# A hybrid decoder layer: value products that read two rows in turn, and tokens copied into residue order

## The chip, the cores and the metric

The kernel runs on one core of a Trainium2 chip. A core has five engines, each of which works through its own list of instructions strictly in order: TensorE (PE; the loading of its stationary operand is shown apart as PEld), VectorE (DVE), ScalarE (ACT), GpSimd (POOL) and SyncE (SP, which here only issues transfers). An instruction may wait for semaphores that other engines or transfers raise; what stands behind it on its list waits with it. SBUF is the on-chip memory that all engines read, PSUM the eight banks in which TensorE accumulates. The metric is the time of one execution on the device, in microseconds, lower is better.

## The reference, cut to what matters

One decoder layer on 512 tokens of width 1024, in float32: half a SwiGLU feed-forward step, a token mixer, and another half feed-forward step, each between RMS norms.

```python
def token_mixer(h, ...):
    proj = h @ w_in                      # all queries, keys, values and gates
    o_nsa = nsa_attention(...)           # 8 heads, 2 key groups: compressed, selected and window branches
    o_dil = dilated_attention(...)       # 12 heads: 3 groups with dilation 1, 4 and 16
    y = sigmoid(g_a) * (o_nsa @ w_nsa_o) + sigmoid(g_b) * (o_dil @ w_dil_o)
    return y @ w_mix_out
```

In `nsa_attention` each head's output is a gated sum of three attentions; each is a product of probabilities and values, `p @ v`. In `dilated_attention` position t of group g reads the tokens t, t-d, t-2d, ... with d = 1, 4 or 16; the groups' outputs are added with weights that come from the softmax denominators of all three.

## The kernel before

**Precision.** Each float32 operand is split into a rounded high part and a low remainder (`split`, L163 on ScalarE and L164 on VectorE); a product is three matmuls, high x high, high x low, low x high (`mm3`, L208 to L210). Weights arrive in `raw` buffers by SP's queue and are split into `whi` and `wlo`, 1024 columns at a time. The tokens stand transposed in `xhl_t`, eight k-tiles of 128 features by 512 tokens, high and low.

**In turn.** With `turn=True` `mm3` reads the moving operand as two rows, the first and second half of its columns, one element of each in turn, and writes the results to the bank one after the other, so that the bank holds the two rows interleaved. Who reads the bank undoes that (`from_turn`). The value products did not do so.

**NSA.** For each of 8 heads and 2 branches the scaled probabilities are transposed to (keys x queries), split, and `hb_values` (L1290) multiplies the value tile of each of four key tiles with them, 512, 384, 256 and 128 queries wide (causal), high and low, into one PSUM bank V. The compressed branch is added by L1364, 512 wide. `fold` (L1298 on ScalarE, L1299 on VectorE) adds the two halves of the bank's partitions into the head's output.

**Dilated attention and the block products.** The dilated scores and softmax rows (L1013, L1014 on TensorE, L1019 on VectorE, L1020 on ScalarE) run between seven-product block multiplications ("P1" to "P7") of the tokens with other columns of `w_in`; a table, PLAN, says how many blocks follow each half head. In the last of four lots P6, P7 and P4 share a T bank in turn: the first has its bank copied to a `ring` buffer by L1539, the second by L1551, and only then P4 may accumulate into the bank on top of it; L1633 keeps P4.

**Dilated values.** The first group's values are projected token tile by token tile (until 632 us) and kept high and low by L1756 and L1757. Groups 2 and 3 need the tokens by residue modulo 4: the projection's stationary operand is `xhl_t` read with a step of four elements, token tile t being residue t. Eight k-tiles, four banks (S, S, T, T), three matmuls each: 96 matmuls 512 wide, which I call the residue stage. During it `factors` computes the groups' weights (L1719 to L1734), and GpSimd scales the dilated probabilities with them (L1747). Then, for each of 4 heads and 3 groups, the probabilities are transposed (L1799 or L1812), split into SP buffers, and multiplied: group 1 by L1826 and L1827 into bank V, copied by L1828; groups 2 and 3 by L1834, 256 columns at a time, added by L1839.

**What sets the order.** The kernel is written as one stream of operations; the framework's scheduler sets the list of each engine by when it reckons operands and buffers are ready. Buffers come from named pools of fixed number: SP has 11 buffers of 128 x 512, used among others for the low parts of splits; a new use waits until all readers of the old one are done.

Of the kernel before, what the change touches and what calls it, by code (L numbers as in the profile page):

```python
# [13 lines left out]
F32R = mybir.dt.float32r  # L14
# [7 lines left out]
P = 128  # L22
D = 1024
S = 512
# [60 lines left out]
class Layer:  # L85
# [110 lines left out]
    def halves(self, v):  # L196

        return v.rearrange("p (h a c) -> p h a c", h=2, a=2)

    def rows_of(self, v):  # L200

# [1084 lines left out]
    def hb_values(self, probs, br, half, out, first):  # L1286
        for kk in range(NT):
            v = self.vn[kk][:, 2 * br + half].rearrange("p h d -> p (h d)")
            for pi, pp in enumerate(probs[kk]):
                self.nc.tensor.matmul(out[:, kk * P:S], v, pp, start=first and kk == 0 and pi == 0, stop=False,  # L1290
                                      skip_group_check=True)

    def fold(self, dst, half, top, bot):

# [6 lines left out]
    def nsa(self, fillers, sums):  # L1301
        nc = self.nc
        pe = self.positions()
        r = self.wcols([(C_KC, 256)])
        src = [r[:, :, 0:P], r[:, :, P:2 * P]]
        r2 = self.wcols([(C_KS, P), (C_KW, P)])
        src2 = [r2[:, :, 0:P], r2[:, :, P:2 * P]]
        early = []
        for s, tag in zip(src + src2, "FFSV"):
            w = None  # L1310
            if tag == "V":
                with self.tc.issue_after(self.scaled[2]), self.tc.issue_after(self.cast_T[1]):
                    w = self.wslots(s, ["SP"] * 4)
            early.append(self.proj_T(s, self.bank(tag), (0, 2 * P), w))
            if len(early) in (2, 3):
                self.pending.pop(0)()
        for n, (b, w) in enumerate(early):
            self.proj_T(None, b, (2 * P, S), w)
        self.positions_T(pe)
        rows = [self.block_rows(b) for b, _ in early[:2]]  # L1320
        kw = early[3][0]
        vw = self.v_weights()
        kparts = [self.k_parts(early[2][0], False)]
        gs = [self.blocks(0, rows[0])]
        kparts.append(self.k_parts(kw, False))
        gs.append(self.blocks(1, rows[1]))
        wq = self.wslots(self.wcols([(0, 64), (256, 64)]), ["Q", "Q", "of", "of"])
        self.v_nsa(vw)
        early = self.hidden_early(0)
        self.oh, self.ol = [], []  # L1330
        heads = [(i, half, br) for i in range(4) for half in range(2) for br in range(2)]
        qs, cmps, ws, live = {}, {}, {}, {}
        probs = {}
        for n in range(len(heads) + LAG):
            if n < len(heads) and n % 4 == 0:
                i = n // 4
                b, _ = self.proj_T(None, None, None, wq) if i == 0 else self.proj_T(self.wcols([(i * 64, 64), (256 + i * 64, 64)]))
                qs[i] = self.q_parts(b)
                if i:
                    cmps[i] = self.cmp_pair(i, qs[i])  # L1340
            m = n - LAG
            if m >= 0:
                i, half, br = heads[m]
                with self.tc.issue_after(self.unit_mm) if m == 0 else ExitStack():
                    probs[m] = self.hb_probs(*live.pop(m), self.gate[:, :, (i + 4 * half) * 3 + 1 + br])
            if n < len(heads):
                i, half, br = heads[n]
                h = i + 4 * half
                if br == 0:
                    ws[h] = self.slot("W")  # L1350
                    nc.vector.tensor_scalar(ws[h], self.dm, -(2.0 ** -(h + 1)), None, op0=OP.mult)
                kb, ka = kparts[br]
                live[n] = self.hb_scores(qs[i][half], ka[half], kb, half, ws[h])
            if m >= 0:
                i, half, br = heads[m]
                with self.tc.issue_after(self.last_pool):
                    sums(m)
                if br == 0:
                    out = self.bank("V")
                    if half == 0:  # L1360
                        of = self.slot("x")
                self.hb_values(probs.pop(m), br, half, out, br == 0)
                if br == 1:
                    nc.tensor.matmul(out, self.vcs[half], cmps[i], start=False, stop=True, skip_group_check=True)  # L1364
                    self.fold(of, half, out[0:64], out[64:128])
                    if half == 1:
                        self.oh.append(of)
            if n < 2:
                self.hidden(n, gs[n], early)
                if n == 0:  # L1370
                    early = self.hidden_early(1)
                else:
                    hid = self.gelu()
            if n == 2:
                self.compressed(hid)
                cmps[0] = self.cmp_pair(0, qs[0])
            fillers()
# [180 lines left out]
    def dil(self, fillers, early_gates):  # L1558
# [216 lines left out]
        for k0 in range(0, KT, 2):  # L1775
            if k0 % 4 == 0:
                r = self.raw(wv[:, k0:k0 + 4], [4, S])
            w = self.wsplit(r[:, k0 % 4:k0 % 4 + 2], [2, S])
            if k0 == 2:
                factors()  # L1780
            for j in range(2):
                xs = [x[k0 + j].rearrange("p (n r) -> p r n", r=4) for x in (self.xh, self.xl)]
                for t in range(NT):
                    self.mm3(banks[t], xs[0][:, t], xs[1][:, t], w[0][:, j], w[1][:, j], k0 + j == 0, k0 + j == KT - 1,
                             turn=True)
# [3 lines left out]
        def value(g, t, hh):  # L1789
            return vt[g][t][:, hh].rearrange("p h d -> p (h d)")  # L1790
# [29 lines left out]
        def values(g, hh, pieces, acc):  # L1820

            mm = nc.tensor.matmul
            if g == 0:
                out = self.bank("V")
                for n, (kk, qc, hi, lo) in enumerate(pieces):
                    mm(out[:, qc], value(g, kk, hh), hi, start=n == 0, stop=False, skip_group_check=True)  # L1826
                    self.last_value = mm(out[:, qc], value(g, kk, hh), lo, start=False, stop=n == NT - 1, skip_group_check=True).ins  # L1827
                nc.scalar.copy(acc, out)  # L1828
                return
            for m, both in enumerate(pieces):  # L1830
                out = self.bank("S")
                for n in range(2):
                    c = slice(n * 256, (n + 1) * 256)
                    self.last_value = mm(out[:, c], value(g, 2 * m + n, hh), both[:, n].rearrange("p x q -> p (x q)"), start=True,  # L1834
                                         stop=True).ins
                av = acc.rearrange("p (n r) -> p n r", r=4)[:, :, 2 * m:2 * m + 2]
                ov = out.rearrange("p (r x n) -> p x n r", r=2, x=2)
                for x in range(2):
                    nc.vector.tensor_add(av, ov[:, x], av)  # L1839

# [362 lines left out]
```

## Time and profile before

| | before |
|---|---|
| median of 3 runs (lowest to highest) | 1083.85 us (1083.21 to 1085.04) |
| profiled execution, its own time | 1083.9 us |
| span in the trace | 1081.8 us |
| TensorE busy, share of the span | 1060.2 us, 98% |
| VectorE busy | 915.0 us, 85% |
| ScalarE busy | 667.9 us, 62% |
| GpSimd busy | 246.4 us, 23% |
| mean granted TensorE clock | 0.999 |

A row of the timeline gives start, duration, engine, line, operation, tiles written and read, size and count, and in brackets the engine's idle time just before and what ended it. A row of the groups gives the line, the operation, its tiles and sizes, the count, the busy time in us and the mean duration in ns, then the idle time before. A row of the waits gives who waited for whom: us in total, how often, the longest. Matmuls overlap in the pipeline, so their pace is read from the distance of their starts and not from their duration.

| stretch, us | what runs | TensorE busy | VectorE | ScalarE |
|---|---|---|---|---|
| 391 to 510 | NSA heads, with projections between | 114.96 of 119 | 94.57 | 85.48 |
| 510 to 600 | dilated scores and block products | 87.72 of 90 | 78.67 | 69.78 |
| 600 to 633 | last blocks, first value projection | 32.44 of 33 | 20.35 | 22.65 |
| 633 to 656 | residue stage | 23.00 of 23 | 12.12 | 8.91 |
| 656 to 700 | dilated value products | 41.59 of 44 | 35.93 | 27.55 |
| 700 to 1082 | gates, mixer output, second feed-forward | 374.80 of 382 | 323.74 | 209.26 |

### The profile page before, as it was taken

How to read it: one execution, taken by the hardware profiler on the slowest of the kernel's cores; microseconds unless marked ns; L12 is line 12 of the kernel's file. 1: busy time of each engine (PE TensorE's matmuls, PEld its weight loads, DVE VectorE, ACT ScalarE, POOL GpSimd, SP SyncE). 2: the span in 40 equal slices, each digit the busy share in tenths (PEclk: the TensorE clock that was granted, in tenths of full speed). 3: DMA queues.
4: the chain of work that ended last, by engine and by line, in shares of the span. 5: the costliest groups of instructions: out<-in, count | busy, mean ns of one | idle time of the engine just before them, and what ended most of it. 6: DMA issues, size and time to landing. Idle time of an engine off the chain costs nothing. (4 is left out here: it accounts for less than half of the span.)

```text
span 1081.8 us, 19360 instructions
## 1 busy us (share of the span) xinstructions
PE 1060.2 (98%) x7166; PEld 974.6 (90%) x7166; DVE 915.0 (85%) x1563; ACT 667.9 (62%) x1196; POOL 246.4 (23%) x345
## 2 busy tenths in 40 slices
PE   9999999999999999999999999999999999999997
PEld 7899999988889977777899998888999999998886
DVE  6999999998787988787996746996888999989775
ACT  7465555567675777676797745754445555668462
POOL 0434445410021054454110039001101111000001
PEclk9999999999999999999999999999999999999999
DMA  9899999999962577886766642574387988579862
GB/s 351 259 273 312 284 299 294 303 315 351 355 225 87 195 263 174 263 187 204 166 196 224 206 119 99 180 263 162 131 276 203 261 248 229 152 248 301 301 203 105
DMA packets 87871, 250.65 MB, mean 232 GB/s; under 512 B 11777, under 2 KB 16993, under 8 KB 85089
## 3 DMA queue, kind: packets, MB, share of 16 engines
q1 hardware_dynamic: 67152, 180.40, 48.4%
q0 software_dynamic: 20192, 68.72, 25.5%
q8 instruction: 56, 0.92, 0.3%
q10 hardware_dynamic: 432, 0.30, 0.1%
q14 instruction: 39, 0.31, 0.1%
HBM read 214.73 MB, written 74.50 MB: 267 GB/s over the span
## 5 line engine op out<-in xcount | busy, mean ns | idle before, releaser
L164 DVE TENSOR_TENSOR wlo<-raw,whi 128x1024 fp32r<-128x1024 f32 (+1 forms) x216 | 261.8, 1217 | 79.9 <-ACT whi L163 77.2
L163 ACT CAST whi<-raw 128x1024 fp32r<-128x1024 f32 (+1 forms) x216 | 223.8, 1040 | 95.3 <-PE pb_F L209 17.2
L208 PE MATMUL pb_F<-xhl_t,whi 128*128 128x256 f32 (+1 forms) x320 | 104.7, 327 | 2.0 <-DVE KA_s L996 1.0
L209 PE MATMUL pb_F<-xhl_t,whi 128*128 128x256 f32 (+1 forms) x320 | 103.1, 322 | 0.0
L210 PE MATMUL pb_F<-xhl_t,wlo 128*128 128x256 f32 (+1 forms) x320 | 103.1, 322 | 0.0
L208 PE MATMUL pb_S<-xhl_t,whi 128*128 128x256 f32 (+1 forms) x280 | 82.2, 294 | 0.0
L209 PE MATMUL pb_S<-xhl_t,whi 128*128 128x256 f32 (+1 forms) x280 | 82.1, 293 | 0.0
L210 PE MATMUL pb_S<-xhl_t,wlo 128*128 128x256 f32 (+1 forms) x280 | 82.1, 293 | 0.0
L229 POOL TENSOR_TENSOR rs_t<-rs_t,mhalf_t 128x1 f32<-128x1 f32 x20 | 13.3, 666 | 249.5 <-DVE rs_t L225 249.5
L208 PEld LDWEIGHTS pb_F<-xhl_t,whi 128*128 128x128 f32 x320 | 61.0, 191 | 6.1 <-issue 1.6
L210 PEld LDWEIGHTS pb_F<-xhl_t,wlo 128*128 128x128 f32 x320 | 61.0, 190 | 3.3
L209 PEld LDWEIGHTS pb_F<-xhl_t,whi 128*128 128x128 f32 x320 | 61.0, 191 | 3.0 <-issue 0.2
L1266 POOL TENSOR_SCALAR SP_s<-SP_s,st_t 128x384 f32<-128x384 f32 (+2 forms) x48 | 49.1, 1053 | 55.5 <-PE pb_T L1232 11.6
L209 PE MATMUL pb_T<-xhl_t,whi 128*128 128x256 f32 x216 | 59.4, 275 | 0.0
L210 PE MATMUL pb_T<-xhl_t,wlo 128*128 128x256 f32 x216 | 59.4, 275 | 0.0
L208 PE MATMUL pb_T<-xhl_t,whi 128*128 128x256 f32 x216 | 59.4, 275 | 0.0
L163 ACT CAST whi<-tmp_t 128x1024 fp32r<-128x1024 f32 x36 | 36.5, 1057 | 30.2 <-DVE tmp_t L582 26.6
L210 PEld LDWEIGHTS pb_S<-xhl_t,wlo 128*128 128x128 f32 x280 | 53.6, 191 | 1.3
L208 PEld LDWEIGHTS pb_S<-xhl_t,whi 128*128 128x128 f32 x280 | 53.6, 191 | 1.3
L209 PEld LDWEIGHTS pb_S<-xhl_t,whi 128*128 128x128 f32 x280 | 53.6, 191 | 1.3
L208 PE MATMUL pb_T<-SP_s,whi 128*128 128x256 f32 x176 | 48.8, 277 | 1.5 <-ACT ring_s L1539 1.0
L210 PE MATMUL pb_T<-SP_s,wlo 128*128 128x256 f32 x176 | 48.7, 277 | 0.0
(930 smaller groups left out, 3713.4 us busy)
## 6 DMA issues: line engine op xcount, KB each, us to landing
raw<-in_gu_dram SPq DMA_DIRECT2D x64, 512.0 KB, 5.8
raw<-tdram SPq DMA_DIRECT2D x40, 512.0 KB, 5.0
PT_s<-in_d_dram POOLq DMA_DIRECT2D x66, 256.0 KB, 6.9
raw<-in_d_dram SPq DMA_DIRECT2D x30, 512.0 KB, 5.1
tdram<-in_d_dram POOLq DMA_DIRECT2D x18, 768.0 KB, 10.4
ldram<-in_w_in_dram POOLq DMA_DIRECT2D x12, 1024.0 KB, 10.5
tdram<-PT_s POOLq DMA_DIRECT2D x44, 256.0 KB, 5.9
raw<-in_w_in_dram SPq DMA_DIRECT2D x11, 1024.0 KB, 4.9
```

What stands on the lines that cost most here:

```text
L163: self.last_cast = self.nc.scalar.copy(dsthi, src).ins
L164: self.last_sub = self.nc.vector.tensor_sub(dstlo, src, dsthi.bitcast(F32)).ins
L208: mm(out, lhi, rhi, start=start, stop=False, skip_group_check=skip)
L209: mm(out, lhi, rlo, start=False, stop=False, skip_group_check=skip)
L210: self.last_mm = mm(out, llo, rhi, start=False, stop=stop, skip_group_check=skip).ins
L229: nc.gpsimd.tensor_tensor(out=r, in0=v, in1=self.mhalf, op=OP.pow)
L1266: self.last_pool = nc.gpsimd.tensor_scalar(pp, pp, st[:, 1, t:t + 1], None, op0=OP.mult).ins
```

## The change

1. **NSA value products in turn.** The moving probabilities of each 128-column token tile are read as two rows of 64 in turn, and the bank V takes them so; `fold` reads the bank with a step of two and writes its output in natural order.
2. **Dilated value products in turn.** Group 1 likewise. For groups 2 and 3 the two 128-wide pieces of a 256-column product are the two rows; the adds read the bank with a step of two.
3. **Tokens copied into residue order.** For each k-tile of the residue stage ScalarE copies the high and the low tokens into an SP buffer each, reading with a step of four elements and writing contiguously: 16 copies of 128 x 512. The 96 matmuls take the copies as their stationary operand.

```diff
+    def tiles_in_turn(self, v):
+        return v.rearrange("p (t a c) -> p t c a", a=2, c=64)
+    def tiles_turned(self, v):
+        return v.rearrange("p (t c a) -> p t c a", a=2, c=64)
+    def tiles_from_turn(self, v):
+        return v.rearrange("p (t c a) -> p t a c", a=2, c=64)
...
-                self.nc.tensor.matmul(out[:, kk * P:S], v, pp, start=first and kk == 0 and pi == 0, stop=False,
-                                      skip_group_check=True)
+                self.nc.tensor.matmul(self.tiles_turned(out[:, kk * P:S]), v, self.tiles_in_turn(pp),
+                                      start=first and kk == 0 and pi == 0, stop=False, skip_group_check=True)
...
-                    nc.tensor.matmul(out, self.vcs[half], cmps[i], start=False, stop=True, skip_group_check=True)
-                    self.fold(of, half, out[0:64], out[64:128])
+                    nc.tensor.matmul(self.tiles_turned(out), self.vcs[half], self.tiles_in_turn(cmps[i]), start=False, stop=True,
+                                     skip_group_check=True)
+                    self.fold(self.tiles(of), half, *[self.tiles_from_turn(out[b:b + 64]) for b in (0, 64)])
...
-                xs = [x[k0 + j].rearrange("p (n r) -> p r n", r=4) for x in (self.xh, self.xl)]
+                xs = []
+                for x in (self.xh, self.xl):
+                    v = self.slot("SP", F32R).rearrange("p (r n) -> p r n", r=4)
+                    nc.scalar.copy(v, x[k0 + j].rearrange("p (n r) -> p r n", r=4))
+                    xs.append(v)
...
-                    mm(out[:, qc], value(g, kk, hh), hi, start=n == 0, stop=False, skip_group_check=True)
-                    self.last_value = mm(out[:, qc], value(g, kk, hh), lo, start=False, stop=n == NT - 1, skip_group_check=True).ins
-                nc.scalar.copy(acc, out)
+                    o, hi, lo = self.tiles_turned(out[:, qc]), self.tiles_in_turn(hi), self.tiles_in_turn(lo)
+                    mm(o, value(g, kk, hh), hi, start=n == 0, stop=False, skip_group_check=True)
+                    self.last_value = mm(o, value(g, kk, hh), lo, start=False, stop=n == NT - 1, skip_group_check=True).ins
+                nc.scalar.copy(self.tiles(acc), self.tiles_from_turn(out))
...
-                    self.last_value = mm(out[:, c], value(g, 2 * m + n, hh), both[:, n].rearrange("p x q -> p (x q)"), start=True,
-                                         stop=True).ins
+                    self.last_value = mm(out[:, c].rearrange("p (q x) -> p q x", x=2), value(g, 2 * m + n, hh),
+                                         both[:, n].rearrange("p x q -> p q x"), start=True, stop=True).ins
...
-                ov = out.rearrange("p (r x n) -> p x n r", r=2, x=2)
+                ov = out.rearrange("p (r n x) -> p x n r", r=2, x=2)
```

The lists of TensorE, GpSimd and SP keep their order; on TensorE the 96 matmuls only read other tiles. What moves is on ScalarE (and on VectorE, where the splits of the NSA outputs come later). ScalarE before, from the last block products on: `whi` are casts of weights, CP_s and CB_s the dilated softmax rows, the first `ring_s` is the copy of P6's bank, L1551 that of P7's, L1633 that of P4's.

```order
L163 CAST whi<-raw 128x1024 x2
L1539 COPY ring_s<-pb_T 128x512
L1020 ACTIVATE CP_s,dst_t<-CP_s,dst_t 128x128 x4
L163 CAST whi<-raw 128x1024
L1020 ACTIVATE CP_s,dst_t<-CP_s,dst_t 128x128 x4
L163 CAST whi<-raw 128x1024
L1551 ACTIVATE ring_s<-pb_T 128x512
L163 CAST whi<-raw 128x1024
L1020 ACTIVATE CB_s,dst_t<-CB_s,dst_t 128x128 x4
L1674 DMA sdram<-dst_t 128x32
L163 CAST whi<-raw 128x1024
L1633 ACTIVATE ring_s<-pb_T 128x512
```

The same stretch of ScalarE in the change (L1020 is now L1036, L1539 L1556, L1551 L1568; L1802 are the new copies):

```order
L163 CAST whi<-raw 128x1024
L1802 COPY SP_s<-xhl_t 128x512 x2
L1556 COPY ring_s<-pb_T 128x512
L163 CAST whi<-raw 128x1024
L1802 COPY SP_s<-xhl_t 128x512 x2
L1036 ACTIVATE CP_s,dst_t<-CP_s,dst_t 128x128 x4
L163 CAST whi<-raw 128x1024
L1802 COPY SP_s<-xhl_t 128x512 x4
L1036 ACTIVATE CP_s,dst_t<-CP_s,dst_t 128x128 x4
L1568 ACTIVATE ring_s<-pb_T 128x512
L163 CAST whi<-raw 128x1024 x2
```

Eight copies, for k-tiles 0 to 3, now stand ahead of P7's copy L1568; one weight cast that stood ahead of it stands behind it.

The second place on ScalarE is the start of the residue stage, before the change and then in it; `fac_t` are the exponentials of `factors` (L1726, now L1743), x_s the splits of the NSA outputs.

```order
L1756 CAST Q_s<-pb_S 128x4x64
L163 CAST whi<-raw 128x1024
L163 CAST x_s<-x_s 128x512 x2
L1726 ACTIVATE fac_t<-fac_t 128x16 x3
L163 CAST x_s<-x_s 128x512
```

```order
L1773 CAST Q_s<-pb_S 128x4x64
L163 CAST whi<-raw 128x1024
L163 CAST x_s<-x_s 128x512
L1802 COPY SP_s<-xhl_t 128x512
L1743 ACTIVATE fac_t<-fac_t 128x16 x3
L1802 COPY SP_s<-xhl_t 128x512 x2
L163 CAST whi<-raw 128x1024
L1802 COPY SP_s<-xhl_t 128x512 x2
```

A copy now stands ahead of the exponentials. It is the twelfth, and the SP pool has 11 buffers, so it waits until k-tile 0's matmuls have read theirs; the second of the four NSA splits stands behind it.

More of the change, by code (lines that the diff above doesn't have):

```diff
@@ L198, in halves, with tiles @@
         return v.rearrange("p (h a c) -> p h a c", h=2, a=2)
+    def tiles(self, v):
+        return v.rearrange("p (t a c) -> p t a c", a=2, c=64)
+    def tiles_in_turn(self, v):
[4 more added lines that the diff above has]
+        return v.rearrange("p (t c a) -> p t a c", a=2, c=64)
     def rows_of(self, v):
```

## The prediction, as put on record

> **What bounds the kernel now.** I read the page's busy row first, then the chain of waits, then TensorE's (PE's) waits stage by stage, and last the order on ScalarE (ACT) where new work is put.
>
> ```profile
> PE 1060.2 (98%) x7166; PEld 974.6 (90%) x7166; DVE 915.0 (85%) x1563; ACT 667.9 (62%) x1196; POOL 246.4 (23%) x345
> PE 33%; DVE 3%; issue 1%; ACT 1%; POOL 1%; DMA 1%; DVEq 0%; POOLq 0%; SPq 0%; ACTq 0%
> PE pb_T L208 <- ACT ring_s L1551: 0.5, 1, 0.5
> PE pb_T L209 <- DVE wlo L164: 0.5, 1, 0.5
> ```
>
> TensorE is busy for 1060.2 of 1081.8 us, and the chain that ends last is mostly TensorE. The third row is one of its waits between 600 and 700 us, the fourth its only listed wait after 700 us. So what TensorE gains or loses before 700 us has no later slack to disappear in: I carry it to the end in full. ScalarE, 62% busy on average, looks free; whether it is free where the sixteen copies go decides the sum.
>
> **Part 3, the gain: contiguous weights in the residue stage.** TensorE start times in the residue stage (640 us), in an ordinary projection (404 us), and the weight loads of the residue stage and of a later stage:
>
> ```profile
> 640.03 0.40 PE L209 MATMUL pb_T<-wlo,xhl_t 128*128 128x512 f32 x1
> 640.27 0.40 PE L210 MATMUL pb_T<-whi,xhl_t 128*128 128x512 f32 x1
> 640.51 0.40 PE L208 MATMUL pb_T<-whi,xhl_t 128*128 128x512 f32 x1
> 404.63 0.38 PE L209 MATMUL pb_F<-xhl_t,whi 128*128 128x512 f32 x1
> 404.84 0.38 PE L210 MATMUL pb_F<-xhl_t,wlo 128*128 128x512 f32 x1
> 405.06 0.38 PE L208 MATMUL pb_F<-xhl_t,whi 128*128 128x512 f32 x1
> L209 PEld LDWEIGHTS pb_S<-wlo,xhl_t 128*128 128x128 f32 x15 | 5.0, 335 | 0.0
> L209 PEld LDWEIGHTS pb_F<-SP_s,whi 128*128 128x128 f32 x4 | 0.8, 189 | 0.1
> ```
>
> Matmuls of the same size follow each other after 0.24 us (0.48 for two) in the residue stage and after 0.215 us (0.43 for two) in the other. Both read the moving operand as two rows in turn; what differs is the stationary operand, read there with a step of four elements, and its load takes 335 ns instead of 189. There are 8 k-tiles x 4 banks x 3 = 96 matmuls, and the stage has no TensorE idle time. Gain: 96 x about 0.021 = **2.0 us**. Should the step not be the cause, the gain is 0.
>
> **Parts 1 and 2, the gain: value products in turn.** The NSA (sparse attention) value products, by size, and a plain 512-wide group and a dilated one:
>
> ```profile
> L1290 PE MATMUL pb_V<-PT_s,V_s 128*128 128x512 f32 x32 | 15.0, 478 | 2.2 <-ACT PT_s L163 1.8
> L1290 PE MATMUL pb_V<-PT_s,V_s 128*128 128x384 f32 x32 | 10.5, 357 | 0.0
> L1290 PE MATMUL pb_V<-PT_s,V_s 128*128 128x256 f32 x32 | 9.1, 319 | 0.0
> L2082 PE MATMUL pb_F<-xhl_t,wlo 128*128 128x512 f32 x8 | 3.2, 394 | 0.0
> L1834 PE MATMUL pb_S<-SP_s,V_s 128*128 128x256 f32 x16 | 3.3, 295 | 0.7 <-DVE SP_s L164 0.7
> ```
>
> A plain 512-wide matmul lasts 394 ns, one in turn 380 (the 404 us rows): 14 to 17 ns apart. Scaled by width that is at most 32 x (17 + 13 + 8) ns = 1.2 us for L1290, 0.1 for the eight compressed products, 0.3 for some 56 products of 256 columns in the dilated part. But L1290's means lie far above the plain group's (478 against 394), so something other than the read order holds part of them; and in the dilated stretch VectorE (DVE) is nearly as full as TensorE. The rows now read 64 elements apart are closer together than in any matmul of the trace that I can put beside them: lower bound 0. I take 0.8 for NSA and 0.2 for the dilated part, **1.0 us**, between 0 and 1.6.
>
> The Trainium skill's "SBUF — State Buffer" (its note on cachelines) states that each access that crosses to another 16-byte line pays a penalty, with two hits per line needed; by that rule reading two far rows in turn should be slow, and parts 1 and 2 would lose. The two groups above deny it for the moving operand (in turn 380 ns, plain 394), so I give it 3 in 100; for the step of four in a weight load the rule and the 335 ns agree.
>
> The other side of the turned layout is reading the bank back with a step of two. For ScalarE two keeps of one size show no price:
>
> ```profile
> L1414 ACT COPY ring_s<-pb_F 128x512 f32<-128x512 f32 x2 | 1.2, 579 | 0.0
> L1828 ACT COPY ring_s<-pb_V 128x512 f32<-128x512 f32 x4 | 2.3, 584 | 0.0
> L1839 DVE TENSOR_TENSOR ring_s<-pb_S,ring_s 128x256 f32<-128x256 f32 x32 | 12.9, 467 | 0.1
> ```
>
> L1414 already reads a turned bank, L1828 a plain one. The adds of L1839 jump 256 elements between neighbours before and after; only the step between their rows changes. Cost: 0.
>
> **Part 3, the cost: sixteen copies on ScalarE.** No copy in the trace reads with this step on this engine. The nearest rows, with the contiguous one of each pair:
>
> ```profile
> L163 ACT CAST x_s<-x_s 128x512 fp32r<-128x512 f32 x6 | 3.7, 618 | 4.4 <-DVE x_s L164 2.2 <-DVE SP_s L164 1.9 <-DVE KB_s L164 0.3
> L458 ACT ACTIVATE W_s<-V_s 128x256 f32<-128x256 f32 x18 | 8.9, 495 | 0.0
> L1224 ACT ACTIVATE SP_s<-SP_s 128x256 f32<-128x256 f32 x4 | 1.6, 402 | 0.0
> L1539 ACT COPY tmp_t<-pb_F 128x512 f32<-128x512 f32 x4 | 2.3, 581 | 0.0
> ```
>
> Contiguous, 512 columns take 0.62 us; the next instruction may start some 0.09 us before the end (rows below: 1.03 us long, successor after 0.94), so the step is c = 0.53 us. L458 reads every other element: 495 against 402 ns for 256, 0.36 ns per element more; on 512 elements c = 0.72. The weight load, at exactly this step of four, pays (335 - 189) / 128 = 1.14 ns per element more: c = 1.11. If its whole 335 / 128 = 2.6 ns per element were the pace, c = 1.4: the upper bound. I take **c = 1.0** (a copy of about 1.1 us), nearer to the row with the same step than to the row with half of it.
>
> What matters is what stands behind the copies. ScalarE in program order before the change, and the TensorE instruction that waits:
>
> ```profile
> 608.18 2.00 ACT L163 CAST whi<-raw 128x1024 fp32r<-128x1024 f32 x2
> 610.21 0.59 ACT L1539 COPY ring_s<-pb_T 128x512 f32<-128x512 f32 x1
> 611.87 0.40 ACT L1020 ACTIVATE CP_s<-CP_s,dst_t 128x128 f32<-128x128 f32 x1 [1.06 <-DVE dst_t L1019]
> 613.42 1.03 ACT L163 CAST whi<-raw 128x1024 fp32r<-128x1024 f32 x1
> 615.96 0.40 ACT L1020 ACTIVATE CP_s<-CP_s,dst_t 128x128 f32<-128x128 f32 x1 [1.50 <-DVE dst_t L1019]
> 617.51 1.03 ACT L163 CAST whi<-raw 128x1024 fp32r<-128x1024 f32 x1
> 618.45 0.59 ACT L1551 ACTIVATE ring_s<-pb_T 128x512 f32<-128x512 f32 x1
> 618.93 1.03 ACT L163 CAST whi<-raw 128x1024 fp32r<-128x1024 f32 x1
> 619.09 0.38 PE L208 MATMUL pb_T<-SP_s,whi 128*128 128x256 f32 x1 [0.54 <-ACT ring_s L1551]
> ```
>
> Block P4 cannot start to accumulate until L1551 has read P7's bank, and TensorE already waits 0.54 us for it. In the change eight copies stand between the first cast of the 608.18 pair and this keep, and the cast at 617.51 stands behind it. Steps from the rows: the cast 0.95, L1539 0.48 (as 618.45 to 618.93), four exponentials 1.55 (611.87 to 613.42). From 608.18: cast 0.95, two copies 2c, L1539 0.48, cast 0.95, two copies, four exponentials 1.55, cast 0.95, four copies, 1.55. The keep starts at 608.18 + 6.43 + 8c = 614.61 + 8c; TensorE follows 0.64 later (618.45 to 619.09), at **615.25 + 8c** instead of 619.09. The idle 1.06 and 1.50 us are used up in that. So the stall is 8c - 3.84: 0.4 us at c = 0.53, 1.9 at 0.72, **4.2 at 1.0**, 5.0 at 1.11, 7.4 at 1.4. TensorE has nothing else queued ahead of P4, so all of it is on the path.
>
> The other eight copies cost nothing more by these rows, and this is what they stand ahead of: ScalarE's DMA of the softmax sums, weight casts, the exponentials of the factors, and the splits of the NSA outputs, whose low parts share the copies' buffers. The factors lead to Pool's scaling of the dilated probabilities, and that to TensorE:
>
> ```profile
> 624.05 0.33 ACTq L1674 DMA_DIRECT2D sdram<-dst_t  x1
> 636.61 0.42 ACT L1726 ACTIVATE fac_t<-fac_t 128x16 f32<-128x16 f32 x3
> 656.49 3.33 POOL L1747 TENSOR_SCALAR x_s<-x_s,gf_t 128x128 f32<-128x128 f32 x4
> 662.07 0.60 PE L1799 MATMUL pb_T<-ident_t,x_s 128*128 128x128 f32 x4
> 655.18 0.40 PE L210 MATMUL pb_T<-whi,xhl_t 128*128 128x512 f32 x1
> 672.52 0.46 PE L208 MATMUL pb_F<-x_s,whi 128*128 128x512 f32 x1
> ```
>
> Pool is done with that tile at 659.82, 2.25 us ahead of TensorE's use. In the change the exponentials stand behind a copy that waits until k-tile 0 of the residue stage is used up: 12 matmuls x 0.215 = 2.6 us after the stage's start. The stage starts 95 x 0.237 us before 655.18, near 632.6; with the stall 636.8; plus 2.6 and c gives 640.4, so 3.8 us late. TensorE comes 4.2 - 2.0 = 2.2 late, and the margin shrinks to about 0.7 us: still hidden. Without it, each microsecond more is one lost. The DMA comes less late: the copy ahead of it waits for P4's last matmuls, about 2.3 us into a block that starts at 623.3, and then takes 1.1: 626.7 in place of 624.05. The splits wait for buffers that k-tiles 2 to 4 free, 13 us into the stage at the latest; their first reader is the last row, at 672.5.
>
> **Sum.** +4.2 - 2.0 - 1.0 = +1.2 us on the profiled execution's own 1083.9 us (span 1081.8, and 2.1 around it), which lies 0.05 above the median of the three runs, 1083.85. Forecast: **1085.1 us**. I call 0.2% (2.2 us) what a measurement of this kernel can tell from no change; this is no change, on the slow side.
>
> **The rivals.**
> *The strided copy is cheap* (c from 0.53 to 0.6, as from a bank). Stall 0.4 to 1.0, sum -2.6 to -2.0: about 1081.5 us, faster. For it: L1539's copies of the F bank read PSUM with a step of four and take 581 ns, no more than plain keeps. Against it: L458 pays from SBUF at half the step. 20 in 100. With c = 0.6 to 0.85 the sum runs from -2.0 to 0.0, near 1083 us: no change, 15 in 100.
> *The copies are dear, P4 waits.* From c = 1.13 the sum passes +2.2; at 1.4 it is 7.4 - 3.0 = +4.4, or 1088.3 us, slower; Pool's margin is then gone too. For it: DVE and PE both lose more at larger steps than L458's 0.36 ns. Against it: it needs more than the weight load's own excess. 23 in 100.
> *Turning gains nothing* (64 elements apart is no faster, or other waits hold these products): with c = 1.0 the sum is +4.2 - 2.0 = +2.2, 1086.1 us, on the edge of slower. 12 in 100, half of it slower.
> *The stationary step isn't what slows the residue stage*: +3.2 us, 1087 us, slower. Against it: 335 against 189 ns. 3 in 100; with the turned reads being slow by lines (3 in 100, at 32 x 3 products a few tenths each, above 1086) the unlikely ways to slower are 6.
>
> **How the numbers follow.** My forecast (c from 0.85 to 1.13, gains as summed, -0.0 to +2.2) has 24 in 100. Faster by over 0.2%: 20 from the cheap copy and 3 from a gain above my sum in the next case, 23. No change: 24 + 12 + 6 = 42. Slower: 23 + 6 + 6 = 35. The range runs from the cheap copy's 1081.3 to the dear one's 1088.3, with one in ten left out on each side; the likeliest case alone spans 1083.9 to 1086.1.
>
> **What would show it.** In the changed trace: the copies' mean duration (1.1 us if I am right, 0.62 if the step is free); TensorE's wait for the ring keep of P7, now about 4.7 us in place of 0.54; residue-stage matmuls 0.215 us apart and weight loads of 189 ns; L1290's 512-wide mean down by some 15 ns; TensorE's waits after 700 us unchanged. I am wrong if the copies cost the contiguous price, if the wait appears at another keep, or if Pool's chain makes TensorE wait at the first dilated transposes.

## The result, and the profile after

| | before | after |
|---|---|---|
| median of 4 runs each, on one chip | 1083.96 us | 1090.99 us |
| lowest to highest | 1083.21 to 1085.04 | 1088.48 to 1091.58 |
| ratio after / before, 95% interval | | 1.0066 (1.0053 to 1.0079) |

The change makes the kernel 7.0 us slower. The forecast was 1085.1 us, called no change on the slow side, with 1088.3 as the upper end of its range: the side was right, and the median lies 2.7 us above that end. The profiled execution of the change is the lowest of its four runs, 1088.48 us.

The page of the change, busy time by engine, and TensorE's waits between 600 and 720 us (us in total, times, longest):

```profile
PE 1057.7 (97%) x7166; PEld 970.7 (89%) x7166; DVE 916.2 (84%) x1563; ACT 687.6 (63%) x1212; POOL 248.2 (23%) x345
...
PE pb_T L224 <- ACT ring_s L1568: 5.5, 1, 5.5
PE pb_T L1820 <- POOL x_s L1764: 2.2, 4, 1.2
```

TensorE is busy 2.5 us less than before and the span is 4.5 us longer: most of the loss is waiting. Two waits have grown: P4's for the keep of P7 (0.5 before) and, at the transposes of the tiles that GpSimd scales (L1820, before L1799), one that the list of before does not have for them.

**The first wait.** The copies by form, ScalarE's order, and P4's first matmuls in the change:

```profile
L1802 ACT CAST SP_s<-xhl_t 128x512 fp32r<-128x512 f32 x16 | 21.0, 1359 | 0.5 <-PE pb_T L225 0.5
...
607.99 2.58 ACT L1802 CAST SP_s<-xhl_t 128x512 fp32r<-128x512 f32 x2
612.03 2.64 ACT L1802 CAST SP_s<-xhl_t 128x512 fp32r<-128x512 f32 x2
617.05 4.11 ACT L1802 CAST SP_s<-xhl_t 128x512 fp32r<-128x512 f32 x4
622.61 0.57 ACT L1568 ACTIVATE ring_s<-pb_T 128x512 f32<-128x512 f32 x1
...
623.24 0.58 PE L224 MATMUL pb_T<-SP_s,whi 128*128 128x256 f32 x1 [5.53 <-ACT ring_s L1568]
623.62 0.42 PE L225 MATMUL pb_T<-SP_s,whi 128*128 128x256 f32 x1
623.83 0.42 PE L226 MATMUL pb_T<-SP_s,wlo 128*128 128x256 f32 x1
```

Eight copies stand between 607.99 and the keep; the instruction behind each group starts 2.61, 2.53 and 4.02 us after it, so a copy's step is 9.16 / 8 = 1.145 us on the mean. After the wait P4's matmuls follow each other 0.21 us apart. Before the change they were 0.11 apart. The windows of the change say why: PEclk, the granted clock, is the third number from the right.

```profile
616.00:619.00 3.00, 1.71 (x16) 1.57 (x15) 1.83 (x8) 3.00 (x5) 0.00 (x0) 1.00 0.00 0
620.00:623.00 3.00, 0.00 (x0) 0.00 (x0) 0.00 (x0) 3.00 (x11) 0.00 (x0) 0.50 0.73 300
624.00:625.00 1.00, 1.00 (x7) 1.00 (x6) 0.84 (x1) 1.00 (x2) 0.00 (x0) 0.50 0.20 67
627.00:628.00 1.00, 1.00 (x11) 1.00 (x10) 0.96 (x9) 0.64 (x3) 0.00 (x0) 1.00 0.98 256
```

While TensorE waits, its clock falls to half, and stays there for the first 3.3 us of P4.

**The second wait.** GpSimd in the change, the row of before that answers to its second, VectorE beside it, and the last transpose of the first lot:

```profile
644.24 0.60 POOL L1764 TENSOR_SCALAR PT_s<-PT_s,fac_t 128x128 f32<-128x128 f32 x1 [57.40 <-DVE fac_t L1751]
646.48 10.57 POOL L1764 TENSOR_SCALAR PT_s<-PT_s,fac_t 128x256 f32<-128x256 f32 x7
658.20 7.65 POOL L1764 TENSOR_SCALAR PT_s<-PT_s,fac_t 128x128 f32<-128x128 f32 x8
665.84 3.23 POOL L1764 TENSOR_SCALAR x_s<-x_s,gf_t 128x128 f32<-128x128 f32 x4
...
646.65 1.42 DVE L164 TENSOR_TENSOR wlo<-raw,whi 128x1024 fp32r<-128x1024 f32 x1 [2.42 <-ACT whi L163]
648.00 0.68 DVE L164 TENSOR_TENSOR SP_s<-x_s 128x512 fp32r<-128x512 f32 x1
...
651.06 1.33 DVE L164 TENSOR_TENSOR wlo<-raw,whi 128x1024 fp32r<-128x1024 f32 x1
...
669.12 0.33 PE L1820 MATMUL pb_T<-ident_t,x_s 128*128 128x128 f32 x1 [0.25 <-POOL x_s L1764]
```

```profile
639.45 0.61 POOL L1747 TENSOR_SCALAR PT_s<-PT_s,fac_t 128x128 f32<-128x128 f32 x1 [51.50 <-DVE fac_t L1734]
641.69 6.56 POOL L1747 TENSOR_SCALAR PT_s<-PT_s,fac_t 128x256 f32<-128x256 f32 x7
649.40 7.11 POOL L1747 TENSOR_SCALAR PT_s<-PT_s,fac_t 128x128 f32<-128x128 f32 x8
```

GpSimd starts 4.8 us later, and the same seven scalings take 10.57 instead of 6.56 us, the eight 7.65 instead of 7.11. So x_s comes 9.35 us later (665.84 against 656.49). Taken singly in the trace, a scaling lasts 0.92 us, and 1.4 to 2.35 where VectorE subtracts one SBUF tile from another at the same time: the weight remainders and the NSA remainders that the copies pushed into this stretch.

**What was gained.** The residue stage and the turned products in the change:

```profile
655.99 0.38 PE L225 MATMUL pb_T<-wlo,SP_s 128*128 128x512 f32 x1
656.20 0.38 PE L226 MATMUL pb_T<-whi,SP_s 128*128 128x512 f32 x1
...
L225 PEld LDWEIGHTS pb_S<-wlo,SP_s 128*128 128x128 f32 x12 | 2.3, 189 | 0.3
...
L1306 PE MATMUL pb_V<-PT_s,V_s 128*128 128x512 f32 x32 | 14.5, 462 | 2.3 <-ACT PT_s L163 1.9
...
L1861 DVE TENSOR_TENSOR ring_s<-pb_S,ring_s 128x256 f32<-128x256 f32 x32 | 13.1, 465 | 0.1
```

The ledger compares the start of one and the same TensorE matmul in the two profiled executions, after minus before:

| up to | difference, us | what the step holds | step |
|---|---|---|---|
| 365 us | -0.87 | the loads at the start; the change does not touch it | -0.9 |
| 504 us | -1.12 | NSA value products in turn | -0.25 |
| P7's start, 612 us | -0.89 | P7's own wait for P6's keep | +0.2 |
| P4's start, 619.09 / 623.24 | +4.15 | wait for the keep of P7 | +5.0 |
| 620.75 / 626.39 | +5.64 | half clock | +1.5 |
| end of the residue stage | +3.65 | contiguous weights | -2.0 |
| 662.39 / 669.12 | +6.73 | wait for GpSimd | +3.1 |
| dilated products | +6.5 | products in turn | -0.2 |
| end | +4.58 | 721 us, 993 to 1002 us: places the change does not touch | -1.9 |

The steps that belong to the change add up to +7.4 us, the difference of the medians is 7.0. The 2.8 us in the first and the last row arise at places that the change does not touch. Against the same trace of before, e10_splits_late, a kernel without copies or turned products, is also 0.8 us ahead by 374 us and gains 0.8 at 721 and 0.3 from 993 to 1002 us.

### The profile page after: what moved, and what is told of

It is laid out like the page before. It is cut to its first block, busy times and chain, and to the rows that moved or that the text cites. A ratio compares the mean times of both kernels' runs of the same rounds, so it can differ in the third digit from the quotient of the medians.

```text
span 1086.3 us, 19381 instructions
## 1 busy us (share of the span) xinstructions
PE 1057.7 (97%) x7166; PEld 970.7 (89%) x7166; DVE 916.2 (84%) x1563; ACT 687.6 (63%) x1212; POOL 248.2 (23%) x345
```

## The experiments

**The halves of the change.** The first kernel has parts 1 and 2 alone; the residue stage reads the tokens with the step of four as before.

```diff
-                    v = self.slot("SP", F32R).rearrange("p (r n) -> p r n", r=4)
-                    nc.scalar.copy(v, x[k0 + j].rearrange("p (n r) -> p r n", r=4))
+                xs = [x[k0 + j].rearrange("p (n r) -> p r n", r=4) for x in (self.xh, self.xl)]
```

> Parts 1 and 2 alone (value products in turn); the residue stage reads the strided tokens as before and there are no copies. Theory A (all of the loss comes from the copies): no wait at P7's keep beyond the 0.5 us of before, clock 0.999, and the time is 0 to 1 us below that of before, because the trace of the change shows TensorE only about 0.25 us ahead after the NSA stretch. Theory B (the turned products lose time somewhere, for instance in the folds or adds that read a bank with a step of two): 2 us or more above before.

1082.46 us, ratio 0.9996 (0.9987 to 1.0005). The wait at the keep is 0.5 us again, the clock full. Turning gains too little to be measured.

The second has part 3 alone: every value product and its read-back as before the change.

> Part 3 alone (the sixteen copies); all value products as before. Theory A: 1090 to 1092 us, as the whole change, with TensorE waiting 5 to 6 us for P7's keep, about 3 us at half clock behind it, and 2 to 3 us of waits for GpSimd's scaling. Theory B: clearly below the whole change, by 2 us or more.

1091.0 us, ratio 1.0081 (1.0064 to 1.0098). The copies hold the whole loss. Its trace has the wait of 5.5 us, GpSimd's waits of 2.2, and half clock twice: after the keep of P7 and again at the dilated transposes, where the change has none.

```profile
620.00:623.00 3.00, 0.00 (x0) 0.00 (x0) 1.09 (x9) 3.00 (x5) 0.00 (x0) 1.00 0.58 158
627.00:630.00 3.00, 3.00 (x16) 3.00 (x16) 2.79 (x11) 0.81 (x5) 0.00 (x0) 0.50 0.44 145
...
673.00:674.00 1.00, 1.00 (x4) 0.82 (x3) 0.54 (x2) 0.37 (x1) 1.00 (x3) 0.50 0.36 88
```

Here nearly all of the lower clock falls on P4's work and what follows it: P4 starts 5.99 us late, and TensorE is 8.67 us late when the clock is full again at 630.7 us, 2.7 us lost. In the change half of the slow time passed while TensorE waited anyway.

**The stride.** The whole change, with the same lists on every engine, but each copy reads its tokens one after the other. This leaves out the residue order, so groups 2 and 3 yield other numbers.

```diff
-                    nc.scalar.copy(v, x[k0 + j].rearrange("p (n r) -> p r n", r=4))
+                    nc.scalar.copy(v, x[k0 + j].rearrange("p (r n) -> p r n", r=4))
```

> The whole change with one thing altered: the copies read the tokens contiguously (so the token tiles of the dilated value projection are not in residue order, and the outputs of its groups 2 and 3 are other numbers); every engine's list is the same as in the change. Theory A, price of the stride: a copy takes 0.62 us, eight of them ahead of P7's keep cost about 4.2 us and the idle time of before covers nearly all: TensorE waits about 1 us there instead of 5.5, no half clock, GpSimd starts about as early as before, and the time is 1081 to 1084 us. Rival (position on the list and buffers, whatever the stride): the wait at P7's keep stays above 3 us and the time above 1087 us.

1082.84 us, ratio 0.9999 (0.9985 to 1.0012). Its copies, its waits, and its clock after the wait:

```profile
L1802 ACT CAST SP_s<-xhl_t 128x512 fp32r<-128x512 f32 x16 | 9.3, 617 | 2.2 <-PE pb_T L225 2.2
...
PE pb_T L224 <- ACT ring_s L1568: 1.6, 1, 1.6
...
621.00:624.00 3.00, 3.00 (x16) 3.00 (x15) 3.00 (x6) 0.71 (x2) 0.00 (x0) 0.50 0.47 161
```

Sixteen copies in the same places at 617 ns lose nothing in sum: the step of the read, 1359 against 617 ns, makes the difference of 7 us. The expectation had no half clock here, and it came after a wait of only 1.6 us: it cost 1.6 us. The wait's +1.0, these 1.6 and the gains of 2.1 and about 0.4 nearly balance.

**The price of a wait alone.** The kernel before, with the keep of P7 done two and four times over; nothing else moves.

```diff
-                nc.scalar.mul(flat(v), src["X"], -1.0)
+                for _ in range(4 if at == 21 else 1):
+                    nc.scalar.mul(flat(v), src["X"], -1.0)
```

> The kernel before, where P7's keep in the last lot is done twice (0.48 us more ahead of P4, nothing else changed). TensorE waits 1.0 us there instead of 0.5. If an idle time of this size does not touch the clock: clock 0.999, and 0.5 us longer than before. If any such wait halves the clock for one period: 0.5 + 1.5 = 2 us longer.

Twice: 1084.31 us, ratio 1.0016 (1.0007 to 1.0025), a wait of 1.2 us and a full clock. P4 starts 0.6 us later in this trace, while the ratio stands for 1.7 us (0.8 to 2.7); whether other executions lost clock behind the same wait is not shown.

> The kernel before, where P7's keep in the last lot is done four times (1.44 us more ahead of P4). TensorE waits 2.0 us. In the run with contiguous copies a wait of 1.6 us was followed by half clock, so: half clock from about 620 us for some 3 us, costing about 1.5 us, in all 1.4 + 1.5 = 2.9 us longer than before. If the half clock belonged to the copies and not to the wait: 1.4 us longer, clock 0.999.

Four times: 1086.47 us, ratio 1.0034 (1.0021 to 1.0047), a wait of 2.4 us. The windows behind its end (620.16 us):

```profile
620.00:622.00 2.00, 1.84 (x8) 1.84 (x9) 1.62 (x2) 1.04 (x2) 0.00 (x0) 0.54 0.52 179
622.00:624.00 2.00, 2.00 (x14) 2.00 (x13) 1.14 (x9) 1.46 (x7) 0.00 (x0) 0.61 0.46 108
```

The clock falls with no copy in the program. A wait 1.9 us longer than before cost 1.9 and, by the starts of the matmuls behind it, 1.6 more for the clock.

**Order.** Can the copies stand where they cost less? In the changed kernel, first the copies of k-tiles 2 to 7 behind the keep of P7, so that four stay ahead of it instead of eight.

```diff
-                    nc.scalar.copy(v, x[k0 + j].rearrange("p (n r) -> p r n", r=4))
+                    with self.tc.issue_after(self.p7_keep) if k0 >= 2 else ExitStack():
+                        nc.scalar.copy(v, x[k0 + j].rearrange("p (n r) -> p r n", r=4))
```

> The whole change, but the copies of k-tiles 2 to 7 are held behind P7's keep, so that four strided copies stand ahead of it instead of eight. By the same adding as in the prediction with 1.3 us a copy the keep starts at about 620.8 in place of 622.6: TensorE waits about 3 us. Theory A with the clock as a price of its own (only an idle time as long as 5.5 us halves the clock): no half clock, wait near 3 us, 1086 to 1088 us if GpSimd's chain stays late, 1084 if not. Rival (the clock drops at any wait of some us): half clock also here.

1089.84 us, ratio 1.0069 (1.0054 to 1.0084), no better than the change; the wait is 4.1 us. ScalarE's list behind the four copies:

```profile
619.45 0.40 ACT L1036 ACTIVATE CP_s<-CP_s,dst_t 128x128 f32<-128x128 f32 x1 [1.50 <-DVE dst_t L1035]
621.00 1.03 ACT L163 CAST whi<-raw 128x1024 fp32r<-128x1024 f32 x1
621.93 0.59 ACT L1568 ACTIVATE ring_s<-pb_T 128x512 f32<-128x512 f32 x1
```

The prediction let copies fill ScalarE's idle 1.50 us. Here that idle time moved along with them: a late weight cast delays VectorE's remainder, the softmax row behind it (L1035) and so the exponentials. TensorE still ran at half clock twice, behind the keep and at the dilated transposes.

Next, twelve copies, none ahead of the keep; k-tiles 0 and 1 are read with the step as before. KA and V are other buffer pools, `vt0_keeps` the keeps of the first value projection, `last_exp` the exponentials of the factors.

```diff
+                    if k < 2:
+                        xs.append(x[k].rearrange("p (n r) -> p r n", r=4))
+                        continue
+                    v = self.slot(("", "KA", "V", "SP")[k // 2], F32R).rearrange("p (r n) -> p r n", r=4)
+                    with self.tc.issue_after((None, self.p7_keep, self.vt0_keeps[0][0], self.last_exp if k >= 2 else None)[k // 2]):
+                        nc.scalar.copy(v, x[k].rearrange("p (n r) -> p r n", r=4))
```

> The turned value products, and copies for k-tiles 2 to 7 alone (12; k-tiles 0 and 1 are read with the step, as before), none ahead of P7's keep: k-tiles 2 and 3 behind that keep into KA buffers, 4 and 5 behind the first value keep into V buffers, 6 and 7 behind the factors' exponentials into SP buffers, so that the NSA splits find SP buffers free. Theory A (the loss was the wait for the keep, the half clock behind it and GpSimd's late chain, not the copies' own time): wait at the keep 0.5 us, clock 0.999, no wait for GpSimd above 0.5 us, gain 72 x 0.021 = 1.5 us in the residue stage and some 0.7 us from the turned products: 1080 to 1082 us. Rival (ScalarE's total work of 12 x 1.35 us between 618 and 650 is itself too much, whatever the order): TensorE waits inside the residue stage and the time is 1084 us or more.

1083.78 us, ratio 1.0004 (0.9994 to 1.0014). The loss is gone; the gain is too:

```profile
PE pb_F L225 <- DVE wlo L164: 0.9, 1, 0.9
...
PE pb_F L224 <- ACT whi L163: 0.4, 1, 0.4
```

Three copies behind the keep stand ahead of a weight cast, and TensorE waits for its two halves at 623 us. By the matmuls' starts this costs 1.8 us, and the stage brought 1.5.

So no copy was left ahead of P4's work: two k-tiles behind P4's keep, four behind the exponentials.

```diff
-                    with self.tc.issue_after((None, self.p7_keep, self.vt0_keeps[0][0], self.last_exp if k >= 2 else None)[k // 2]):
+                    with self.tc.issue_after(self.p4_keep if k < 4 else self.last_exp):
```

> The turned value products and twelve copies as in the run with twelve placed copies, but those of k-tiles 2 and 3 stand behind P4's keep (and so behind the weight casts of the first value projection, which waited there for copies), and those of k-tiles 4 to 7 behind the factors' exponentials. Theory A: the 1.2 us of new waits at 623 us go; residue stage 1.5 us shorter, no half clock, the time 1081.0 to 1082.5 us, 1 to 2 us below before. Rival (eight copies of 1.55 us on end in the stage come too late for k-tiles 5 to 7, or GpSimd's chain is late again): TensorE waits of a microsecond or more inside the stage or at the dilated transposes, time as before or above.

1084.33 us, ratio 1.0012 (1.0002 to 1.0023). No wait at 623, and the stage gains 1.5 us. Then TensorE waits at the first transposes:

```profile
PE pb_T L1839 <- POOL x_s L1764: 2.4, 1, 2.4
...
658.07 0.74 DVE L1774 TENSOR_TENSOR V_s<-pb_T,V_s 128x256 fp32r<-128x256 f32 x2
...
658.63 1.72 PE L1839 MATMUL pb_T<-ident_t,PT_s 128*128 128x128 f32 x7 [2.39 <-POOL x_s L1764]
```

The list names GpSimd, but what releases TensorE is VectorE's last value keep, which must empty the T bank: before the change, in it and here TensorE starts 0.22 us after the second of the two keeps does. The first stands at 658.07 us, where it stood before (658.12), behind a weight remainder. TensorE arrives early and waits, and the wait brings half clock, 1.7 us.

Last, eight copies: k-tiles 2 to 5 alone, the fourth pair left out of the copies.

```diff
-                    if k < 2:
+                    if k < 2 or k >= 6:
```

> The turned value products, and copies for k-tiles 2 to 5 alone (8; k-tiles 0, 1, 6 and 7 are read with the step), placed as in the run before this one: k-tiles 2 and 3 behind P4's keep, 4 and 5 behind the factors' exponentials. Gain in the residue stage 48 x 0.021 = 1.0 us, and some 0.7 us from the turned products. Theory A (what is left to pay is what a copy pushes later: without the last four the NSA splits and the value keeps come as early as before): wait at the first dilated transposes back to 0.5 us, no half clock, 1081.5 to 1082.5 us, below before. Rival (strided copies on ScalarE cost as much as they bring wherever they stand): within 0.5 us of before or above.

1082.82 us, ratio 1.0000 (0.9989 to 1.0012). The stage gains 1.0; the wait for the value keep (`PE pb_T L1839 <- DVE V_s L1774`) grows to 0.9 us and other short ones follow. They take the gain back.

**GpSimd and VectorE.** The kernel before without any copy, its NSA splits held behind the factors, as in the change.

```diff
-            with self.tc.issue_after(kept[0]), self.tc.issue_after(kept[1]):
+            with self.tc.issue_after(self.fac_done), self.tc.issue_after(kept[1]):
```

> The kernel before with one edit: the four splits of the NSA outputs are held behind the factors, so that their VectorE parts (0.68 us each, two operands in SBUF) run while GpSimd scales the probabilities, as in the change, with no copies at all. Theory (VectorE's SBUF work holds GpSimd up): GpSimd's scaling operations that meet one take about 1.5 to 2 us instead of 0.92, its chain reaches the first tile of group 2 about 2 us later, and TensorE's margin of 2.25 us there is nearly used up; time within 1 us of before. Rival (GpSimd was slowed by ScalarE's strided copies, not by VectorE): durations and chain as before, to 0.3 us.

1082.99 us, ratio 0.9997 (0.9987 to 1.0007). GpSimd's first scalings:

```profile
636.83 1.08 POOL L1747 TENSOR_SCALAR PT_s<-PT_s,fac_t 128x128 f32<-128x128 f32 x1 [49.67 <-DVE fac_t L1734]
639.55 8.83 POOL L1747 TENSOR_SCALAR PT_s<-PT_s,fac_t 128x256 f32<-128x256 f32 x7
```

8.83 us against 6.56 before: moving the splits alone, without a copy, makes these scalings 2.3 us longer, where the change makes them 4.0 longer. It costs no time here, and not because the margin was used up: with the splits out of their way the factors, and so GpSimd, were 2.6 us early (636.83 against 639.45), and x_s came at 656.65, nearly where it came before. The expected delay of 2 us at that tile did not come.

**Another engine.** First the twelve copies placed as in e5_twelve_copies_placed, with those of k-tiles 0 and 1 added on GpSimd (buffers KA, V and SP in turn).

```diff
+                    if k < 2:
+                        nc.gpsimd.tensor_copy(v, x[k].bitcast(F32).rearrange("p (n r) -> p r n", r=4))
```

> As the run with twelve placed copies, and the four copies of k-tiles 0 and 1 on GpSimd, which is idle from about 590 to 639 us (KA buffers; k-tiles 2 and 3 go to V, 4 to 7 to SP). Prices the strided copy on GpSimd: if it takes under 3 us, k-tile 0 is there when the residue stage starts, the whole 2.0 us are gained and the time is about 0.5 us below the other run's. If it takes 4 us or more, TensorE waits at the start of the residue stage, and GpSimd's scaling starts late.

1086.36 us, ratio 1.0025 (1.0014 to 1.0036). A copy takes GpSimd 1.09 to 1.37 us. The full 2 us are gained in the stage; waits of 1.2 at the keep, 0.9 and 0.4 at 623, 1.1 for V_s and 0.7 for x_s take more. The time is 2.6 us above the other run's, where 0.5 below was expected.

Then fourteen copies, k-tiles 0 to 6, all on GpSimd, k-tile 7 read with the step; ScalarE's and VectorE's lists are those of before.

```diff
-                    nc.scalar.copy(v, x[k0 + j].rearrange("p (n r) -> p r n", r=4))
+                    v = self.slot(("SP", "SP", "SP", "KA", "KA", "V", "V")[k], F32R).rearrange("p (r n) -> p r n", r=4)
+                    nc.gpsimd.tensor_copy(v, x[k].bitcast(F32).rearrange("p (n r) -> p r n", r=4))
```

> The turned value products, and the copies of k-tiles 0 to 6 (14) on GpSimd instead of ScalarE, into SP, KA and V buffers as these come free from 607 us on; k-tile 7 is read with the step. ScalarE's list holds no copies and is in the order of before; the NSA splits find SP buffers free. Four such copies on GpSimd took 1.1 to 1.4 us each. Theory A (the copies themselves are harmless where an idle engine makes them): wait at P7's keep 0.5 us, no half clock, GpSimd done with the copies by 635 us and its scaling on time, residue stage 84 x 0.021 = 1.8 us shorter, of which the keeps and the dilated part may take back up to 1: 1080.5 to 1082.5 us, the fastest version, ratio about 0.998. Rival (GpSimd and VectorE hold each other up in SBUF, as in the run with late splits): VectorE's weight remainders between 607 and 635 us come late, TensorE waits for them or for P7's keep by 1 us or more, and the time is 1084 us or above.

1086.37 us, ratio 1.0033 (1.0019 to 1.0047). VectorE's weight remainders in its trace, the exponentials that wait for it, and TensorE:

```profile
615.55 2.06 DVE L164 TENSOR_TENSOR wlo<-raw,whi 128x1024 fp32r<-128x1024 f32 x1 [1.42 <-ACT whi L163]
...
617.86 0.40 ACT L1036 ACTIVATE CP_s<-CP_s,dst_t 128x128 f32<-128x128 f32 x1 [2.34 <-DVE dst_t L1035]
...
PE pb_T L224 <- ACT ring_s L1568: 2.7, 1, 2.7
```

A remainder takes 1.23 us on the mean before; of the five that run beside GpSimd's copies three take 2.0 to 2.3. So the same chain (remainder, softmax row, exponentials, keep) is late without one copy on ScalarE, and half clock follows again (1.6 us).

## Why the prediction was wrong

| term of the sum | predicted, us | measured, us |
|---|---|---|
| residue stage, contiguous weights | -2.0 | -2.0 |
| NSA and dilated products in turn | -1.0 | -0.45 |
| read-back of turned banks | 0 | 0 (L1861 465 ns, before 467) |
| eight copies ahead of P7's keep, 8c - 3.84 | +4.2 | +5.3 |
| clock behind the wait | no term | +1.5 |
| GpSimd's chain, "still hidden" | 0 | +3.1 |
| sum | +1.2 | +7.4 |

**Right: the residue stage.** 0.215 us apart, loads of 189 ns, 2.0 us, as worked out from the two rows with equal moving operands.

**Right in place, short in size: the copies.** The wait came at the keep that was named, and the formula holds: with the measured step c = 1.145 it gives 5.3 us (5.0 at P4, 0.2 at P7). The step that failed is "I take c = 1.0". The weight load with the same step of four had said 1.11, and it was shaded towards the row with half the step. The mean also hides two prices: the first four copies, beside TensorE's matmuls, took 1.285 us each, the last four, with TensorE almost wholly at rest, 1.005. So 1.0 was near the price of a copy beside an idle TensorE, which no row that the prediction used could tell apart. One part of the formula is only fortunate: e4_copies_behind_keep shows that the idle 1.06 and 1.50 us on ScalarE are not simply there to be filled, since VectorE's softmax rows wait for the casts that copies delay. With eight copies the row was done in time, so it made no difference.

**Wrong: no term for the clock.** "the stall is 8c - 3.84 ... all of it is on the path" ended the account of the wait at its end. The clock had been 0.999 in the trace of before, whose wait there is 0.54 us, so nothing spoke of it; e8_keep_four_times shows that a wait alone brings it.

**Wrong: "the margin shrinks to about 0.7 us: still hidden".** One of the prediction's own signs of being wrong, a wait for GpSimd's chain at the first dilated transposes, came true. The work was expected 3.8 us late and came 9.35 late; TensorE was expected 2.2 late and came 3.65 late. Of the 9.35, 4.8 are the later start, not far from the 3.8. The other 4.55 are scalings that ran longer, for which there was no term: the splits were followed to their reader at 672.5 us and no further, though VectorE's part of them moved into the stretch in which GpSimd works. A margin of 2.25 us against a sum of uncertain delays deserved a price in the range, which its own sentence gave ("without it, each microsecond more is one lost") and the sum did not use.

**Wrong in size: the turned products.** The 512-wide mean fell by 16 ns, as forecast (about 15), and all of L1306's busy time by 1.1 us. But starts moved by 0.25 us only: a matmul's modelled duration overlaps with the next one's, so 32 x 16 ns was not 0.5 us of time. In the residue stage the gain had been taken from the starts, and was exact.

**The rivals.** "The copies are dear, P4 waits" had the mechanism, the place and the point (c = 1.13), and even that GpSimd's margin would be gone; at the measured c its price was 5.3 - 3.0 = +2.3 us. What it lacked is the same two terms, 4.6 us together. "Turning gains nothing" is nearly right and is not the cause. "The stationary step isn't what slows the residue stage" and "reading two far rows in turn is slow" are refuted by the ledger.

**Left open.** What of GpSimd's 4.0 us in the change comes from the weight remainders rather than the moved splits was not tried apart; in e10_splits_late, too, its slow scalings met both. Two runs with small losses, e6_gpsimd_first_copies and e12_copies_on_gpsimd, have profiled executions below their medians (1084.19 and 1083.97 us), so their traces show the waits but not the whole of the loss.

## What to carry to other kernels

Price a wait of the bounding engine as the wait plus what its clock loses behind it; here a wait from 1.6 us on cost another 1.5 to 2.7. When work is put into gaps of a half-idle engine, follow everything that moves with it to the end: the engines that will now work at the same time, not only the readers that will now wait. Take gains of pipelined matmuls from the distance of their starts, and a gain of 2 us only for real once the next stage's operands are ready 2 us earlier too.

## What the runs showed of the hardware that was not expected

**The clock.** Waits of TensorE of 1.6, 2.4, 2.7, 4.1 and 5.5 us were followed by half clock, waits of 0.5 and 1.2 us were not. Half clock lasted 3.4 us in e3_contiguous_read, e8_keep_four_times, e9_no_copy_before_stage_work and e12_copies_on_gpsimd, 6.8 in the change, and 6.8 and later 3.4 in e2_copies_only and e4_copies_behind_keep. In all fourteen traces the clock changes only at the marks of a grid of 3.413 us, which lies differently in each execution: in e2_copies_only half clock begins at 623.90 and again at 671.69 us, 14 such periods apart. The windows can be cut along the grid (TensorE's busy time stands behind the comma, PEclk is the third number from the right). At the dilated transposes, first the change, then e2_copies_only:

```profile
664.05:667.47 3.42, 2.50 (x11) 1.56 (x9) 1.41 (x3) 1.53 (x2) 3.42 (x6) 1.00 0.11 46
667.47:670.88 3.41, 2.09 (x11) 1.74 (x12) 1.10 (x3) 0.74 (x2) 3.41 (x6) 1.00 0.12 26
670.88:674.29 3.41, 3.41 (x28) 3.25 (x28) 1.63 (x5) 1.26 (x4) 3.41 (x7) 1.00 0.82 224
```

```profile
668.28:671.69 3.41, 1.42 (x6) 0.61 (x4) 1.22 (x1) 1.53 (x2) 3.41 (x5) 1.00 0.00 0
671.69:675.11 3.42, 3.21 (x9) 2.47 (x9) 0.85 (x2) 0.74 (x2) 3.42 (x7) 0.50 0.26 78
```

The same four short waits of 2.2 us in sum fall into two periods in the change, 0.9 and 1.3 us idle, and mostly into one in e2_copies_only, 2.0 us idle; only there half clock follows. So it is in all traces: of the periods at full clock, the nine with 1.55 us of idle time or more are followed by half clock, and none with 1.33 us or less is. It also explains why the change lost 1.5 us of its 6.8 and e2_copies_only 2.7 after equal waits: half clock began 3.6 us ahead of P4's start in the one and 1.2 us in the other. No run set the grid's place on purpose, and the idle times rest on modelled ends of matmuls. The Trainium skill's "TensorE: Matmul & The Clock Gate" (Part 1) states a free-running window of about 3.4 us, which agrees with the grid; its rule that gaps above about 3.4 us are to be avoided is too lax for this case, where a wait of 1.6 us was enough.

**A strided read by ScalarE depends on TensorE.** The same copy of 128 x 512 with a step of four takes 1.08 to 1.13 us in the change while TensorE stands almost or wholly still (617 to 621 us), 1.30 to 1.38 beside 256-wide matmuls, 1.55 to 1.58 beside the 512-wide ones of the residue stage; a contiguous one (e3_contiguous_read) takes 0.60 to 0.63 beside either kind of matmul. In e4_copies_behind_keep four copies beside 256-wide matmuls at half clock take 1.12 to 1.15. So the price of a strided read taken from one stretch does not carry to another.

**GpSimd and VectorE hold each other up.** Scalings of 0.92 us became 1.4 to 2.35, remainders of 1.23 up to 2.0 to 2.3, GpSimd's copies of 1.1 to 1.4 us up to 2.1 to 2.4, each only where the other engine worked from SBUF to SBUF. The Trainium skill's "SBUF — State Buffer" (SBUF: two separate sides) states that the two share a port pair, which one holds for a whole instruction while the other is blocked; these rows agree.
